# A two-layer trunk on one core: the seven products of each MLP weight pair put side by side, and the tiles of x and its sums moved in on-chip memory

## The chip, the cores and the metric

One core of a Trainium2 chip runs the whole program in one launch. The metric is the device time of one execution in microseconds (us), and of several executions the median. Nothing crosses cores, and the weights come from HBM once.

The engines are named as the profile names them. PE multiplies matrices; PEld is its weight load, which runs beside it. DVE and POOL do elementwise work, ACT applies functions and casts, and SP only issues loads and stores.

## The reference

Two layers work on 512 tokens of 1024 features. Each is a mixer (gated delta rule in the first, sliding-window attention in the second, both beside a small cross-attention) and an MLP. The change touches the MLP above all; the rest is shown by its names alone.

```python
def sq_relu_mlp(h, w_up, w_down):                  # h 512x1024, w_up 1024x4096, w_down 4096x1024
    return jnp.square(jax.nn.relu(h @ w_up)) @ w_down

def reference(x, mem, positions, a_w_in, ..., mlp_w_up, mlp_w_down, ln_g, ln_b):
    ...
    for layer in range(DEPTH):                     # DEPTH = 2
        mix = mixer_a(...) if layer < N_A else mixer_b(...)
        h = layer_norm(DN_ALPHA * h + mix, ln_g[layer, 0], ln_b[layer, 0])
        h = layer_norm(DN_ALPHA * h + sq_relu_mlp(h, mlp_w_up[layer], mlp_w_down[layer]), ...)
        if layer == N_A - 1:
            k_sh, v_sh = shared_kv(h, w_kv_shared, cos, sin)
    return h
```

## The kernel before, in words

**Split operands.** Every large matmul runs on numbers split into a high part (a cast to a shorter float, on ACT) and a low part (what is left, a subtraction on DVE). A product is then three matmuls: high by high, low by high, high by low. `wload` (line 81) loads a weight tile `wr` and splits it into `wh` and `wl`; `split_copy` (line 117) does the same for a tile that is there already. The activations stand in `XH` and `XL`, with features on the partitions. In a row `out<-a,b` of the views, one of a, b is the stationary operand (its 128 columns are loaded by PEld) and the other is the moving one (its 256 or 512 columns stream through PE).

**The MLP.** `mlp` (line 777) runs once per layer. The 4096 hidden features fall into eight chunks of 512, and a chunk into two pairs of 128-feature tiles. `ups_first` computes the first chunk, `ups_second` half of the second, and the 13 pairs that remain are objects of `Pair`, so there are 26 in the program. A pair multiplies a 2 by 2 arrangement of weight blocks by a 2 by 2 arrangement of x blocks with seven block products in place of eight. `x_sums` (line 833) builds the three sums of x blocks once per layer, as the split tiles `TH` and `TL`; `up_load` (line 854) loads a pair's two weight tiles and builds four weight sums `sa`, `sb` on POOL.

**The seven products.** `product` (line 865) issues 12 matmuls, 4 blocks of 128 features by 3, each with 256 moving columns. The results gather in three accumulators, `upa`, `upb` and `upd`, and a product that adds onto one of them may start only when the sum that has to read it before is done. That sets the order: m1 (opens `upa`), m6 (opens `upb`), then the sum u2 on DVE, m2 (onto `upa`), m5 (opens `upd`), m7 (onto `upb`), then the sums u3 and r22, m4 (onto `upb`), the sum r21, m3 (onto `upd`), the sum r12. m1, m2, m5 and m3 read `XH` and `XL`; m6, m7 and m4 read `TH` and `TL`. m4's weights are `w2h` and `w2l`, a small tile of their own; the other weights are `wh` and `wl`. `close` applies relu and square and splits the result into `hh` and `hl`.

**The downs.** `down` (line 938) multiplies an earlier chunk's `hh`, `hl` by a slab of the second weight matrix for one tile of 128 tokens: 12 matmuls of 512 moving columns into a bank `dn`, of which there are three, and one DVE addition onto `res`. A pair comes with four downs.

**The order of the work.** Each engine runs its queue in order. The loop in `mlp` gives the order of PE: m1, m6, m2, m5, m7, down 0, m4, down 1, m3, down 2, down 3. A scheduler may put elementwise work on the other engines earlier than the code does: the splits of the next pair (`split0` for the first weight tile, `split_b` and `split_a` for `sb` and `sa`, `split2` for `w2h`) stand between the current pair's sums. Weight tiles come in a ring of four `wr` and five `wh`, `wl`, so a load on SP waits until the tile that it overwrites has been split.

Of the kernel before, what the change touches and what calls it, by code (L numbers as in the profile page):

```python
# [11 lines left out]
F32 = mybir.dt.float32  # L12
# [6 lines left out]
P = 128  # L19
# [30 lines left out]
def trunk(ctx: ExitStack, tc: tile.TileContext, xT, xn, memT, wk, wq, wv, wqm, wz, wmk, wmv, wo0, wo1, up, dn,  # L50
# [15 lines left out]
    def ct(shape, tag, dt=F32):  # L66
        return cp.tile(shape, dt, tag=tag, name=tag)
# [7 lines left out]
    def fr(ap):  # L75
        return ap.bitcast(F32)
# [4 lines left out]
    def wload(src, shape):  # L81
# [6 lines left out]
        V.tensor_sub(lo, raw, fr(hi))  # L88
        return hi, lo

    XH = ct([P, KT, S], "XH", F32R)
    XL = ct([P, KT, S], "XL", F32R)
    res = ct([P, NT, D], "res")
    lns = ctx.enter_context(tc.tile_pool(name="lns", bufs=2))
    wa_stack = ExitStack()
    wpool[0] = wa_stack.enter_context(tc.tile_pool(name="wa", bufs=3))
# [19 lines left out]

    def split_copy(src, hi, lo):
        A.copy(hi, src)  # L118
        V.tensor_sub(lo, src, fr(hi))  # L119

    def split_scores(ps, q, k):

# [26 lines left out]
    triu = c0([P, P], "triu")  # L149
    G.affine_select(triu, ones, [[1, P]], ALU.is_ge, 0.0, base=0, channel_multiplier=-1)  # L150
    slow = c0([P, P], "slow", F32R)
    slow32 = c0([P, P], "slow32")
    G.affine_select(slow32, ones, [[-1, P]], ALU.is_gt, 0.0, base=0, channel_multiplier=1)
    V.tensor_copy(slow, slow32)
    mtri = c0([P, P], "mtri")
    G.memset(mtri, 0.0)
    G.affine_select(mtri, mtri, [[1, P]], ALU.is_ge, NEG, base=0, channel_multiplier=-1)
    band = ct([P, 256], "band")
# [8 lines left out]
    convw = ct([P, 18, 4], "convw")  # L167
    gbT = ct([P, 4, 2, KT], "gbT")

    def row_bcast(src, n, tag):  # L170
        t = ct([P, n], tag)
        SY.dma_start(t, src.rearrange("(o n) -> o n", o=1).broadcast_to([P, n]))
        return t

# [40 lines left out]
    SY.dma_start(gbT, lngb)  # L215
    alog_b = row_bcast(alog, NH, "alog_b")
    dtb_b = row_bcast(dtb, NH, "dtb_b")
    nw_b = row_bcast(nw, P, "nw_b")
    sink_b = row_bcast(sinks, 12, "sink_b")
    invf_b = row_bcast(invf, 32, "invf_b")  # L220
    pos_i = ct([P, NT], "pos_i", I32)
# [20 lines left out]
            if gates is not None:  # L242
                V.tensor_copy(gates[:, :, t], ps[:, n:n + 12])

    ab = ct([P, 12, NT], "ab")
    proj_z(2, ab)


    gg = [ct([P, 24], f"gate{i}") for i in range(12)]
    (ga, gb_, ge, gs, gs2, gacc, g_, beta, eg, neg, egl, gt) = gg  # L250

    def v6(t):
# [19 lines left out]
    for n in (13, 11, 9, 7, 5, 3, 1):  # L272
# [9 lines left out]
    gsp = [ct([P, 24], f"gsplit{i}", F32R) for i in range(2)]  # L282
    split_copy(g_, *gsp)
    ps = smt("v6ps")
    T.matmul(ps[:, 0:24], triu, g_, start=True, stop=True)
# [491 lines left out]
    def mlp(pool, layer, last, gb0):  # L777
# [5 lines left out]
        def f4(shape, n):  # L783
            return pool.tile(shape, F32, tag="f4", name=nm(n), bufs=5)

        def split(raw, shape, tag="wh"):
# [4 lines left out]
            split_copy(raw, hi, lo)  # L791
            return hi, lo

        def hidden(r, hh, hl):
# [38 lines left out]
        def x_sums():  # L833
            q = lambda k, t: (XH[:, k, t], XL[:, k, t])
            x11, x12, x21, x22 = q(kA, tA), q(kA, tB), q(kB, tA), q(kB, tB)
            t1 = f4([P, 4, HT], "t1")
            if layer == 0:
                f11, f12, f21, f22 = (xf[j][:, :, t] for j in range(2) for t in (tA, tB))
            else:
                f11, f12, f21, f22 = t1, *(f4([P, 4, HT], n) for n in ("f12", "f21", "f22"))  # L840
                for f, x in ((f11, x11), (f12, x12), (f22, x22), (f21, x21)):
                    V.tensor_tensor(f, fr(x[0]), fr(x[1]), op=ALU.add)
            V.tensor_sub(t1, f12, f11)
            V.tensor_sub(f12, f22, f12)
            V.tensor_sub(f22, f22, t1)
            V.tensor_sub(f21, f21, f22)
            TH, TL = (pool.tile([P, 3, 4, HT], F32R, tag=n, name=nm(n), bufs=1) for n in ("TH", "TL"))
            for i, t in enumerate((f22, f12, f21)):
                split_copy(t, TH[:, i], TL[:, i])

            xq.update(t1=t1, B11=x11, B21=x21, B22=x22, T1=x12,
                      **{n: (TH[:, i], TL[:, i]) for i, n in enumerate(("T2", "T3", "T4"))})
# [9 lines left out]
            G.tensor_tensor(sb[:, 1], raw[0][:, kB], sb[:, 0], op=ALU.subtract)  # L862
            return raw, sa, sb

        def product(ps, w, x, start, stop):
            (hi, lo), (mh, ml) = w, x
            for k in range(4):
                T.matmul(ps, hi[:, k, :], mh[:, k, :], start=start and k == 0, stop=False, skip_group_check=True)  # L868
                T.matmul(ps, hi[:, k, :], ml[:, k, :], start=False, stop=False, skip_group_check=True)  # L869
                T.matmul(ps, lo[:, k, :], mh[:, k, :], start=False, stop=stop and k == 3, skip_group_check=True)  # L870

        class Pair:
# [23 lines left out]

            def m1(self):
                self.a = smt("upa")[:, 0:HT]
                product(self.a, self.A11, xq["B11"], True, False)
                self.s1 = self.small("m1")  # L900
                A.copy(self.s1, self.a)

# [11 lines left out]
            def m7(self):  # L914
                product(self.b, self.S3, xq["T3"], False, False)
                self.u3 = self.small("u3")
                V.tensor_tensor(self.u3, self.s1, self.b, op=ALU.add)
                V.tensor_tensor(self.r[:, 1, tB], self.u3, self.d, op=ALU.add)

            def m5(self):  # L920
                self.d = smt("upd")[:, 0:HT]
                product(self.d, self.S1, xq["T1"], True, False)

            def m4(self):
                product(self.b, self.A22, xq["T4"], False, True)
# [48 lines left out]
        for c in range(NC - 1):  # L974
            later = new_hid()
            for n in range(2):
                p, nxt = nxt, None
                first = c == 0 and n == 0
                f0 = 4 * c + 2 * n + 6
                if first:  # L980
                    ups_second(later)
                    slabs = dn_slabs(c, n)
                else:
                    p.m1()
                    p.m6()
# [282 lines left out]
```

## Time and profile before

| | |
|---|---|
| time, median of 3 runs | 1182.09 us (1181.24 to 1185.84) |
| the profiled execution, its time and its span | 1183.56 us and 1181.8 us |
| ACT busy | 559.3 us (47%) |
| POOL busy | 220.7 us (19%) |
| weights read from HBM | 109.53 MB |
| mean granted clock of PE | 0.991 |

The span runs from the first to the last instruction; the time is 1.8 us longer. A matmul's busy time includes its way through the array, so that busy times of matmuls in a row overlap: how fast PE really goes is read from the distance between starts. The MLP of the first layer fills about 340 to 655 us of the span, that of the second about 840 to 1150 us; the mixers fill the rest.

### The profile page before, as it was taken

To read this page: it belongs to the slowest core of one execution; us is meant where nothing else is said; L and a number is where in the kernel's file an instruction comes from. 1 tells how busy PE (TensorE), PEld (TensorE's weight loads), DVE (VectorE), ACT (ScalarE), POOL (GpSimd) and SP (SyncE) were. 2 spreads that over 40 slices of the span, in tenths; PEclk is the share of its full clock that TensorE was granted. 3 is DMA by queue.
4 is the path that set the end of the run, shared out by engine and by line. 5 is a ranking of instruction groups with operands and counts; after the bars stand their busy time and mean duration, and the time that the engine had idled before them with its cause. 6 is when DMAs were issued, how large, how long until landed. Compare 5 with 4: busy or idle time off the path is not lost.

```text
span 1181.8 us, 18955 instructions
## 1 busy us (share of the span) xinstructions
PE 1153.5 (98%) x7470; PEld 1013.4 (86%) x7470; DVE 857.4 (73%) x1606; ACT 559.3 (47%) x1008; POOL 220.7 (19%) x180
## 2 busy tenths in 40 slices
PE   8999999999999999999999999999999999999996
PEld 8877788879998899898998887778988998989985
DVE  5478889777698676666666968886986666666657
ACT  6345454755384354544435236652653545444341
POOL 0112111101005322313110100000053223131104
PEclk9999999999999999999999999999999999999998
DMA  7522141203423323242333241102342232423311
GB/s 254 180 72 79 61 133 39 68 19 114 154 68 125 112 89 126 72 141 74 106 110 92 70 135 62 55 19 72 108 136 97 89 125 72 140 75 108 107 36 71
DMA packets 40729, 114.16 MB, mean 97 GB/s; under 512 B 11136, under 2 KB 12032, under 8 KB 40640
## 3 DMA queue, kind: packets, MB, share of 16 engines
q1 hardware_dynamic: 40064, 112.04, 29.4%
q8 instruction: 58, 0.95, 0.3%
q10 hardware_dynamic: 576, 0.92, 0.2%
q14 instruction: 31, 0.25, 0.1%
HBM read 109.53 MB, written 3.41 MB: 96 GB/s over the span
## 4 chain that ended last, share of the span: by engine, by line
PE 83%; DVE 10%; ACT 3%; DMA 1%; POOL 1%; issue 1%; POOLq 0%; SPq 0%; ACTq 0%; DVEq 0%
PE dn L113 9%; PE dn L114 9%; PE dn L112 9%; PE upb L868 3%; PE upb L869 3%; PE upb L870 3%; PE wo L114 2%; PE wo L112 2%; PE wo L113 2%; PE upa L869 2%; PE upd L869 2%; PE upa L870 2%; PE upd L870 2%; PE upa L868 2%; PE upd L868 2%; PE up L103 2%
## 5 line engine op out<-in xcount | busy, mean ns | idle before, releaser
L114 PE MATMUL dn<-wh,hl 128*128 128x512 f32 x512 | 200.0, 391 | 0.0
L113 PE MATMUL dn<-wl,hh 128*128 128x512 f32 x512 | 200.0, 391 | 0.0
L112 PE MATMUL dn<-wh,hh 128*128 128x512 f32 x512 | 199.6, 390 | 0.0
L87 ACT CAST wh<-wr 128x1024 fp32r<-128x1024 f32 (+1 forms) x136 | 142.5, 1051 | 104.4 <-PE dn L114 25.0
L88 DVE TENSOR_TENSOR wl<-wr,wh 128x1024 fp32r<-128x1024 f32 (+1 forms) x136 | 166.4, 1226 | 34.1 <-ACT wh L87 31.7
L947 DVE TENSOR_TENSOR res<-res,dn 128x512 f32<-128x512 f32 x120 | 82.1, 684 | 53.8 <-PE dn L114 53.7
L114 PEld LDWEIGHTS dn<-wh,hl 128*128 128x128 f32 x512 | 96.1, 188 | 20.3
L112 PEld LDWEIGHTS dn<-wh,hh 128*128 128x128 f32 x512 | 96.4, 188 | 17.6
L113 PEld LDWEIGHTS dn<-wl,hh 128*128 128x128 f32 x512 | 96.1, 188 | 17.7
L859 POOL TENSOR_TENSOR sa<-wr 128x512 f32<-128x512 f32 x26 | 39.2, 1506 | 373.8 <-DMA wr<-in_up_dram 306.2
L653 POOL TENSOR_TENSOR rs<-rs,nhalf 128x1 f32<-128x1 f32 x16 | 13.3, 833 | 334.9 <-DVE rs L652 267.7
L118 ACT CAST wh<-sa 128x1024 fp32r<-128x1024 f32 x26 | 27.3, 1050 | 90.2 <-PE upd L869 90.2
L119 DVE TENSOR_TENSOR wl<-wr,wh 128x1024 fp32r<-128x1024 f32 x26 | 33.0, 1268 | 43.9 <-ACT wh L118 43.9
L869 PE MATMUL upa<-XL,wh 128*128 128x256 f32 x208 | 58.5, 281 | 0.0
L869 PE MATMUL upd<-XL,wh 128*128 128x256 f32 x208 | 58.5, 281 | 0.0
L870 PE MATMUL upa<-XH,wl 128*128 128x256 f32 x208 | 58.4, 281 | 0.0
L870 PE MATMUL upd<-XH,wl 128*128 128x256 f32 x208 | 58.3, 280 | 0.0
L868 PE MATMUL upa<-XH,wh 128*128 128x256 f32 x208 | 58.3, 280 | 0.0
L868 PE MATMUL upd<-XH,wh 128*128 128x256 f32 x208 | 58.2, 280 | 0.0
L868 PE MATMUL upb<-TH,wh 128*128 128x256 f32 x208 | 58.0, 279 | 0.0
L869 PE MATMUL upb<-TL,wh 128*128 128x256 f32 x208 | 57.8, 278 | 0.0
L870 PE MATMUL upb<-TH,wl 128*128 128x256 f32 x208 | 57.6, 277 | 0.0
(402 smaller groups left out, 3296.7 us busy)
## 6 DMA issues: line engine op xcount, KB each, us to landing
wr<-in_up_dram SPq DMA_DIRECT2D x64, 512.0 KB, 4.8
wr<-in_dn_dram SPq DMA_DIRECT2D x64, 512.0 KB, 4.3
wr<-in_wo_dram SPq DMA_DIRECT2D x16, 512.0 KB, 3.6
wr<-in_bw_dram SPq DMA_DIRECT2D x8, 512.0 KB, 4.5
wr<-in_wz_dram SPq DMA_DIRECT2D x6, 520.0 KB, 4.4
wr<-in_wk_dram SPq DMA_DIRECT2D x6, 512.0 KB, 3.7
wr<-in_wq_dram SPq DMA_DIRECT2D x6, 512.0 KB, 3.6
wr<-in_wv_dram SPq DMA_DIRECT2D x6, 512.0 KB, 3.6
```

The costliest lines, as they stand in the source:

```text
L87: A.copy(hi, raw)
L88: V.tensor_sub(lo, raw, fr(hi))
L112: T.matmul(ps, sh, hi[:, kk, :], start=(k == 0), stop=False)
L113: T.matmul(ps, sh, lo[:, kk, :], start=False, stop=False)
L114: T.matmul(ps, sl, hi[:, kk, :], start=False, stop=(k == nk - 1))
L118: A.copy(hi, src)
L119: V.tensor_sub(lo, src, fr(hi))
L859: G.tensor_tensor(sa[:, 0], raw[1][:, kA], raw[1][:, kB], op=ALU.add)
L868: T.matmul(ps, hi[:, k, :], mh[:, k, :], start=start and k == 0, stop=False, skip_group_check=True)
L869: T.matmul(ps, hi[:, k, :], ml[:, k, :], start=False, stop=False, skip_group_check=True)
L870: T.matmul(ps, lo[:, k, :], mh[:, k, :], start=False, stop=stop and k == 3, skip_group_check=True)
L947: V.tensor_tensor(dst, dst, ps, op=ALU.add)
```

## The change

Four things change.

1. **Order of the products.** All seven run one after the other (m1, m6, m2, m7, m5, m4, m3), and then the four downs. The sum r22 moves from `m7` to `m5`, which now comes later.
2. **The first split of the next pair.** `split0` may not go ahead of r22 on DVE any more: `behind` adds an order between the two, without a semaphore.
3. **Places in memory.** Small unused tiles (`pad0` to `pad4`) and the move of some small mixer tiles to the other end of the memory shift the large tiles. The table has, for the tiles that PE reads, the start in a partition's bytes, as the program's allocation has it, divided by 256: the remainder.
4. **A copy of the first block of x.** Once per layer ACT copies the 256 columns of `XH` that m1 reads first into a tile `x0`, and the first matmul of each m1 reads that copy. Its remainder differs from that of `XH` by 32.

| tile | remainder before | after |
|---|---|---|
| `XH`, `XL`, `res` | 128 | 160 |
| `TH`, `TL` | 160 | 160 |
| `wh`, `wl` of the MLP | 224 | 224 |
| `w2h`, `w2l` | 160 | 224 |
| `hh`, `hl` | 224 | 224 |
| `x0` | none | 128 |
| `MH`, `ML` (memory tokens, at the start) | 224 | 224 |
| the four `wh` of the first mixer | 32, 224, 160, 96 | 32, 224, 160, 96 |

Since every step inside these tiles that a matmul's start takes is a multiple of 256, the remainder holds for all blocks of a tile.

```diff
+    ct([P, 8], "pad0")
     XH = ct([P, KT, S], "XH", F32R)
     XL = ct([P, KT, S], "XL", F32R)
     res = ct([P, NT, D], "res")
+    ct([P, 56], "pad1")
...
     def split_copy(src, hi, lo):
         A.copy(hi, src)
-        V.tensor_sub(lo, src, fr(hi))
+        return V.tensor_sub(lo, src, fr(hi))
+
+    def behind(ins, first):
+
+        if first is not None:
+            tc.add_manual_dep(ins.ins, first.ins.name,
+                              mybir.DependencyInfo(mybir.DependencyClass.NoSync, mybir.DependencyReason.DATA),
+                              reason="order")
...
     slow = c0([P, P], "slow", F32R)
-    slow32 = c0([P, P], "slow32")
-    G.affine_select(slow32, ones, [[-1, P]], ALU.is_gt, 0.0, base=0, channel_multiplier=1)
-    V.tensor_copy(slow, slow32)
     mtri = c0([P, P], "mtri")
+    G.affine_select(mtri, ones, [[-1, P]], ALU.is_gt, 0.0, base=0, channel_multiplier=1)
+    V.tensor_copy(slow, mtri)
     G.memset(mtri, 0.0)
...
-    ab = ct([P, 12, NT], "ab")
+    ab = c0([P, 12, NT], "ab")
...
             for i, t in enumerate((f22, f12, f21)):
                 split_copy(t, TH[:, i], TL[:, i])
+
+            pool.tile([P, 40], F32, tag="pad3", name=nm("pad3"), bufs=1)
+            xq["first"] = pool.tile([P, HT], F32R, tag="x0", name=nm("x0"), bufs=1)
+            pool.tile([P, 24], F32, tag="pad4", name=nm("pad4"), bufs=1)
+            A.copy(xq["first"], fr(XH[:, 0, tA]))
...
-        def product(ps, w, x, start, stop):
+        def product(ps, w, x, start, stop, first=None):
             (hi, lo), (mh, ml) = w, x
             for k in range(4):
-                T.matmul(ps, hi[:, k, :], mh[:, k, :], start=start and k == 0, stop=False, skip_group_check=True)
+                m = mh[:, k, :] if k or first is None else first
+                T.matmul(ps, hi[:, k, :], m, start=start and k == 0, stop=False, skip_group_check=True)
...
-            def split0(self):
-                hi, lo = split(self.raw[0], [P, KT, P])
+            def split0(self, first):
+                hi, lo = split(self.raw[0], [P, KT, P], first=first)
...
                     p.m2()
+                    p.m7()
                     p.m5()
-                    p.m7()
+                    p.m4()
+                    p.m3()
+                    p.close(later)
...
                 down(c, 0, n, hid, slabs)
-                if not first:
-                    p.m4()
                 if nxt:
-                    nxt.split0()
+                    nxt.split0(None if first else p.r22)
                 down(c, 1, n, hid, slabs)
-                if not first:
-                    p.m3()
-                    p.close(later)
```

The tables below show rows of the built programs; lines are those of each kernel's own source, so `L868` before is `L884` after, and `L112` is `L115`.

On PE, at the end of m7 in the sixth pair of the first layer, before: the last matmuls of m7 (`upb`), then down 0.

```order
L868 MATMUL upb_4820<-TH_3703,wh_4787 128x256
L869 MATMUL upb_4820<-TL_3704,wh_4787 128x256
L870 MATMUL upb_4820<-TH_3703,wl_4788 128x256
L112 MATMUL dn_4903<-wh_4841,hh_4213 128x512
L113 MATMUL dn_4903<-wl_4842,hh_4213 128x512
L114 MATMUL dn_4903<-wh_4841,hl_4214 128x512
```

The same place in the change: m7 ends, and m5 (`upd`) follows at once.

```order
L884 MATMUL upb_4826<-TH_3704,wh_4793 128x256
L885 MATMUL upb_4826<-TL_3705,wh_4793 128x256
L886 MATMUL upb_4826<-TH_3704,wl_4794 128x256
L884 MATMUL upd_4885<-XH,wh_4793 128x256
L885 MATMUL upd_4885<-XL,wh_4793 128x256
L886 MATMUL upd_4885<-XH,wl_4794 128x256
```

Where m1 begins, the change has `x` (the copy) in the place of `XH`, in one matmul of the twelve.

```order
L116 MATMUL dn_4797<-wl_4658,hh_4219 128x512
L117 MATMUL dn_4797<-wh_4657,hl_4220 128x512
L884 MATMUL upa_4811<-x_502_3714,wh_4757 128x256
L885 MATMUL upa_4811<-XL,wh_4757 128x256
L886 MATMUL upa_4811<-XH,wl_4758 128x256
```

On DVE, the same pair from the sum u2 on, before: u2 (`L907`), `split0` of the next pair (`wl<-wr`), u3 and r22 (`L917`, `L918`), `split_b`, the addition of down 0, r21 (`L926`), and so on.

```order
L907 TENSOR_TENSOR u_665_4833<-m_663_4818,upb_4820 128x256
L119 TENSOR_TENSOR wl_4931<-wr_4893,wh_4930 128x1024
L917 TENSOR_TENSOR u_676_4890<-m_663_4818,upb_4820 128x256
L918 TENSOR_TENSOR r_4863<-u_676_4890,upd_4865 128x256
L119 TENSOR_TENSOR wl_4966<-sb_4898,wh_4965 128x1024
L947 TENSOR_TENSOR res<-res,dn_4903 128x512
L926 TENSOR_TENSOR r_4863<-m_663_4818,upb_4820 128x256
L119 TENSOR_TENSOR w2l_5250<-wr_5112,w2h_5249 128x512
L947 TENSOR_TENSOR res<-res,dn_4934 128x512
L930 TENSOR_TENSOR r_4863<-u_665_4833,upd_4865 128x256
L119 TENSOR_TENSOR wl_4984<-sa_4897,wh_4983 128x1024
```

After: the three sums u2, u3, r22 stand together, `split0` comes behind them, and the additions of the downs come behind all five sums.

```order
L923 TENSOR_TENSOR u_669_4839<-m_667_4824,upb_4826 128x256
L933 TENSOR_TENSOR u_679_4883<-m_667_4824,upb_4826 128x256
L938 TENSOR_TENSOR r_4869<-u_679_4883,upd_4885 128x256
L122 TENSOR_TENSOR wl_4954<-wr_4929,wh_4953 128x1024
L942 TENSOR_TENSOR r_4869<-m_667_4824,upb_4826 128x256
L122 TENSOR_TENSOR wl_4972<-sb_4934,wh_4971 128x1024
L946 TENSOR_TENSOR r_4869<-u_669_4839,upd_4885 128x256
L122 TENSOR_TENSOR wl_4990<-sa_4933,wh_4989 128x1024
L963 TENSOR_TENSOR res<-res,dn_4939 128x512
L122 TENSOR_TENSOR w2l_5256<-wr_5148,w2h_5255 128x512
L122 TENSOR_TENSOR hl_4614<-r_4869,hh_4613 128x1024
```

On ACT the cast of `w2h` moves from ahead of the relu to behind the square, in 22 pairs; the other engines' queues hold the same work in the same order, but for the two copies and the mask `mtri` at the start.

More of the change, by code (lines that the diff above doesn't have):

```diff
@@ L168, in trunk, with row_bcast @@
     gbT = ct([P, 4, 2, KT], "gbT")
-    def row_bcast(src, n, tag):
-        t = ct([P, n], tag)
+    def row_bcast(src, n, tag, where=ct):
+        t = where([P, n], tag)
         SY.dma_start(t, src.rearrange("(o n) -> o n", o=1).broadcast_to([P, n]))
@@ L217, in trunk @@
     dtb_b = row_bcast(dtb, NH, "dtb_b")
-    nw_b = row_bcast(nw, P, "nw_b")
+    nw_b = row_bcast(nw, P, "nw_b", c0)
     sink_b = row_bcast(sinks, 12, "sink_b")
@@ L243, in proj_z @@
                 V.tensor_copy(gates[:, :, t], ps[:, n:n + 12])
-    ab = ct([P, 12, NT], "ab")
+    ab = c0([P, 12, NT], "ab")
     proj_z(2, ab)
-    gg = [ct([P, 24], f"gate{i}") for i in range(12)]
+    gg = [c0([P, 24], f"gate{i}") for i in range(12)]
     (ga, gb_, ge, gs, gs2, gacc, g_, beta, eg, neg, egl, gt) = gg
@@ L281, in trunk @@
                            op0=ALU.mult, op1=ALU.mult)
-    gsp = [ct([P, 24], f"gsplit{i}", F32R) for i in range(2)]
+    gsp = [c0([P, 24], f"gsplit{i}", F32R) for i in range(2)]
     split_copy(g_, *gsp)
@@ L784, in f4, with split @@
             return pool.tile(shape, F32, tag="f4", name=nm(n), bufs=5)
-        def split(raw, shape, tag="wh"):
+        def split(raw, shape, tag="wh", first=None):
             small = tag != "wh"
@@ L790, in split @@
             lo = wp.tile(shape, F32R, tag=tag[:-1] + "l", name=nm(tag[:-1] + "l"), bufs=n)
-            split_copy(raw, hi, lo)
+            behind(split_copy(raw, hi, lo), first)
             return hi, lo
@@ L847, in x_sums @@
             TH, TL = (pool.tile([P, 3, 4, HT], F32R, tag=n, name=nm(n), bufs=1) for n in ("TH", "TL"))
+            pool.tile([P, 16], F32, tag="pad2", name=nm("pad2"), bufs=1)
             for i, t in enumerate((f22, f12, f21)):
                 split_copy(t, TH[:, i], TL[:, i])
+            pool.tile([P, 40], F32, tag="pad3", name=nm("pad3"), bufs=1)
+            xq["first"] = pool.tile([P, HT], F32R, tag="x0", name=nm("x0"), bufs=1)
+            pool.tile([P, 24], F32, tag="pad4", name=nm("pad4"), bufs=1)
+            A.copy(xq["first"], fr(XH[:, 0, tA]))
             xq.update(t1=t1, B11=x11, B21=x21, B22=x22, T1=x12,
@@ L898, in m1 @@
                 self.a = smt("upa")[:, 0:HT]
-                product(self.a, self.A11, xq["B11"], True, False)
+                product(self.a, self.A11, xq["B11"], True, False, xq["first"])
                 self.s1 = self.small("m1")
@@ L917, in m7 @@
                 V.tensor_tensor(self.u3, self.s1, self.b, op=ALU.add)
-                V.tensor_tensor(self.r[:, 1, tB], self.u3, self.d, op=ALU.add)
             def m5(self):
@@ L922, in m5 @@
                 product(self.d, self.S1, xq["T1"], True, False)
+                self.r22 = V.tensor_tensor(self.r[:, 1, tB], self.u3, self.d, op=ALU.add)
             def m4(self):
```

## The prediction

> **What bounds the kernel now.** I read the page first: the span, the shares of the engines, the granted clock by slices, and the chain of waits.
>
> ```profile
> span 1181.8 us, 18955 instructions
> PE 1153.5 (98%) x7470; PEld 1013.4 (86%) x7470; DVE 857.4 (73%) x1606; ACT 559.3 (47%) x1008; POOL 220.7 (19%) x180
> PEclk9999999999999999999999999999999999999998
> PE 83%; DVE 10%; ACT 3%; DMA 1%; POOL 1%; issue 1%; POOLq 0%; SPq 0%; ACTq 0%; DVEq 0%
> ```
>
> PE is busy 98% of the span at a full clock, and 83% of the chain is PE itself. So taking waits away can bring little; a large gain has to make PE faster at the same 7470 matmuls. Whether there is room is read from the distance between starts. The groups give the counts, the timeline of one late pair the distances.
>
> ```profile
> L112 PE MATMUL dn<-wh,hh 128*128 128x512 f32 x512 | 199.6, 390 | 0.0
> L868 PE MATMUL upa<-XH,wh 128*128 128x256 f32 x208 | 58.3, 280 | 0.0
> L102 PE MATMUL kq<-XH,wh 128*128 128x512 f32 x96 | 38.5, 401 | 0.0
> L102 PE MATMUL up<-XH,wh 128*128 128x256 f32 x128 | 36.0, 282 | 0.0
> L112 PE MATMUL projqMM<-wh,XH 128*128 128x512 f32 x64 | 25.9, 405 | 0.0
> L102 PE MATMUL up<-XH,wh 128*128 128x512 f32 x32 | 12.7, 396 | 0.0
> ```
>
> ```profile
> 376.77 0.28 PE L868 MATMUL upa<-XH,wh 128*128 128x256 f32 x1
> ...
> 605.72 0.28 PE L868 MATMUL upa<-XH,wh 128*128 128x256 f32 x1
> ...
> 607.14 0.28 PE L868 MATMUL upb<-TH,wh 128*128 128x256 f32 x1
> ...
> 608.51 0.28 PE L868 MATMUL upa<-XH,wh 128*128 128x256 f32 x1
> ...
> 609.92 0.28 PE L868 MATMUL upd<-XH,wh 128*128 128x256 f32 x1
> ...
> 611.33 0.28 PE L868 MATMUL upb<-TH,wh 128*128 128x256 f32 x1
> ...
> 612.72 0.39 PE L112 MATMUL dn<-wh,hh 128*128 128x512 f32 x1
> ...
> 615.46 0.28 PE L868 MATMUL upb<-TH,w2h 128*128 128x256 f32 x1
> ...
> 616.88 0.39 PE L112 MATMUL dn<-wh,hh 128*128 128x512 f32 x1
> ...
> 619.65 0.28 PE L868 MATMUL upd<-XH,wh 128*128 128x256 f32 x1
> ...
> 621.08 0.39 PE L112 MATMUL dn<-wh,hh 128*128 128x512 f32 x1
> ...
> 623.81 0.39 PE L112 MATMUL dn<-wh,hh 128*128 128x512 f32 x1
> ...
> 626.53 0.28 PE L868 MATMUL upa<-XH,wh 128*128 128x256 f32 x1
> ```
>
> Eleven pairs begin between 376.77 and 605.72, at 20.81 us each, and the next takes 20.81 too: every pair is alike, and none has a gap. Within a pair each product is twelve equal matmuls, yet m1 takes 1.42 us, m6 1.37, m2 1.41, m5 1.41, m7 1.39, m4 1.43, m3 1.43: 9.86 in all. The two that read TH with a `wh` tile are the shortest. The downs take 2.74, 2.77, 2.73 and 2.72.
>
> The only thing in the tables that goes with it is the pair of remainders. XH at 128 with weights at 224 gives 1.41 / 12 = 117.5 ns from start to start; TH at 160 with 224 gives 1.37 / 12 = 114.2, the way in included; `w2h` at 160 with TH at 160, together with the way in from a down, 1.43 / 12 = 119. The start of the program has the same products with other remainders:
>
> ```profile
> 14.54 0.28 PE L114 MATMUL VM<-wh,ML 128*128 128x256 f32 x1
> ...
> 16.66 0.28 PE L112 MATMUL VM<-wh,MH 128*128 128x256 f32 x1
> ...
> 18.32 0.28 PE L104 MATMUL KM<-MH,wl 128*128 128x256 f32 x1
> ...
> 19.52 0.28 PE L102 MATMUL KM<-MH,wh 128*128 128x256 f32 x1
> 19.88 0.28 PE L102 MATMUL KM<-MH,wh 128*128 128x256 f32 x1
> ...
> 22.48 0.28 PE L104 MATMUL KM<-MH,wl 128*128 128x256 f32 x1
> ```
>
> KM's line is one loop. While its weights lie at 224, as MH does, ten steps take 1.20 us (120 ns); from the buffer at 160 on, 23 steps take 2.60 (113). So 113.3 is what PE can do (12 of them 1.36 us), and equal remainders cost 6.7 ns a matmul. VM is a warning: its weights at 32 differ from ML's 224 by an odd multiple of 64, as TH from `wh`, and still 18 steps take 2.12 (117.8). A fitting difference is thus not enough; the stream must also fall into step, and TH's products, which come behind a product at another remainder, do.
>
> **The change part by part.**
>
> *Places of XH and w2.* They take XH to TH's remainder, so that m1, m2, m5 and m3 meet `wh` as m6 and m7 do, and take `w2h` to where `wh` lies. This operation is not in the trace: no XH product at 160. Bounds: 113.3 ns at best, 120 at worst (KM at equal remainders). I take 113.3, since TH with `wh` has both remainders of the new case.
>
> *All seven products contiguous.* There is then one way in per pair, at m1, from a down. `x0`, 32 away, is read by the first matmul only. Its price is not shown; the nearest row is m7, which comes from XH to TH and takes 1.39 against 1.36, so 0.03; bounds 0 and 0.07 (m4, from a down). The downs follow one another: the second and the third lose 0.05 and 0.01, and the first keeps its 0.02.
>
> New pair: 7 x 1.36 + 0.03 + 4 x 2.72 + 0.02 = 20.45. Gain 0.36 each, 26 x 0.36 = 9.4 us.
>
> *XH elsewhere.* The first chunk's matmuls and the second's, of the second layer:
>
> ```profile
> 849.73 0.28 PE L104 MATMUL up<-XH,wl 128*128 128x256 f32 x1
> ...
> 851.14 0.28 PE L104 MATMUL up<-XH,wl 128*128 128x256 f32 x1
> ...
> 859.70 0.40 PE L102 MATMUL up<-XH,wh 128*128 128x512 f32 x1
> ...
> 862.51 0.40 PE L102 MATMUL up<-XH,wh 128*128 128x512 f32 x1
> ```
>
> Twelve steps take 1.41 and 2.81, against 1.36 and 2.72: 4.2 and 7.5 ns a matmul. The group of 128 stands for 3 x 128 / 2 = 192 matmuls in one layer: 0.8 us. I count one layer, since PE idles in the first one's. The group of 32 stands for 96: 0.7. In the mixers kq has 288 and projq 192 at about 7.5 ns too, 2.2 and 1.4 us at most, but their weights change remainder from buffer to buffer; bounds 0 and 3.6, and I take 1.4.
>
> *The sums.* Four products in a row on one accumulator leave less time to the sums between. From DVE's timeline:
>
> ```profile
> 381.19 0.41 DVE L907 TENSOR_TENSOR u<-m,upb 128x256 f32<-128x256 f32 x1
> ...
> 608.78 0.42 DVE L907 TENSOR_TENSOR u<-m,upb 128x256 f32<-128x256 f32 x1 [0.18 <-PE upb L870]
> 611.09 1.23 DVE L119 TENSOR_TENSOR wl<-wr,wh 128x1024 fp32r<-128x1024 f32 x1 [1.88 <-ACT wh L118]
> 612.92 0.42 DVE L917 TENSOR_TENSOR u<-m,upb 128x256 f32<-128x256 f32 x1 [0.60 <-PE upb L870]
> ```
>
> u2 ends at 609.20; m7, which waits for it, would now start at 605.72 + 0.03 + 3 x 1.36 = 609.83: 0.63 to spare. u3 ends 0.62 behind the last start of m7 (613.34 against 612.72), and m4 comes one product later, 1.36: 0.74 to spare, and r22 before m3 likewise. These hold only if DVE is free at that time: the 1.23 us of `split0` between u2 and u3 would use all of it, and the new order keeps it out. The first pair is the exception: u2 ends at 381.60 there, and m7 would start at 376.77 + 4.11 = 380.88, a stall of 0.7 us. In the second layer's first pair I expect at most that, and take 0.
>
> *Behind `split0`.* It ended at 612.32, 6.6 us into the pair; behind r22 (612.55 + 0.62) it ends at about 614.4, 8.7 in. SP's next load of that tile, which waits for it, goes 2 us later, and all loads behind it in SP's queue. What reads the load is POOL:
>
> ```profile
> 449.59 1.30 POOL L859 TENSOR_TENSOR sa<-wr 128x512 f32<-128x512 f32 x1 [13.64 <-DMA wr<-in_up_dram]
> ...
> 471.93 1.87 DVE L119 TENSOR_TENSOR w2l<-wr,w2h 128x512 fp32r<-128x512 f32 x1
> ```
>
> It stands 10.4 us into the fourth pair (376.77 + 3 x 20.81 = 439.20). At 12.4, four such sums end by 17.6, inside the pair, and the splits of `sa` and `sb` stand behind the sums of the pair that follows. No PE wait is seen: I cost this at nothing. ACT's cast of `w2h`, moved behind the square, precedes its use by most of a pair; the copies into `x0` are two, ahead of 26 pairs: nothing.
>
> Sum: -9.4 - 0.8 - 0.7 - 1.4 + 0.7 = -11.6 us. On the profiled execution, 1183.56 (span 1181.8 and 1.8 around it), that is 1172.0; it lies 1.5 above the median of the runs, from which it would be 1170.5. I say 1171.
>
> **The rivals.**
>
> *Places do nothing here (it doesn't do what it says).* The distances would then come from something that moves with the order, and stay: only the 0.7 of the first pair remains, 1183. Against it: KM, where only the weight buffer changes. The Trainium skill, in "SBUF — State Buffer", section "SBUF: two separate sides", says that on the engines' side only the port pair shared by DVE and GpSimd causes contention and that PE never waits; by that rule no place could matter. KM's 120 and 113 ns speak against it here. In "TensorE: Matmul & The Clock Gate", section "Wait — 56ns, not 53.3ns?", it has a fixed cost of about 2.5 ns per matmul on N / 2.4 GHz, which gives an estimate of 109.2 ns for 256 columns; no row here reaches it.
>
> *Partial: XH's products stay out of step,* as VM does at a fitting difference. Then only m4 (0.07) and the downs (0.06) gain: 26 x 0.13 = 3.4, less 0.7: 1179. For it: VM. Against: all of m6 and m7.
>
> *Wrong step, the slower side.* If the row of 84 locks at the 120 ns of KM's first part, it has no product at another remainder in it any more to leave that state: 84 x 0.120 = 10.08 against 9.86, +0.22, downs -0.06, 26 x 0.16 = 4.2; the first chunk 192 x 2.5 ns, 0.5; the stall 0.7. Together +5.4: 1187.5. With the downs' gain it decides at (9.86 + 0.06) / 84 = 118.1 ns a matmul: from there on the pair is longer than before. For it: one wrong way in is carried through the whole row, where now each change of operand ends it.
>
> *DVE late at u2.* POOL's sums stretch DVE's work: w2l took 1.87 where half of the 1.23 would be 0.62. One such stretch ahead of u2, from 0.63 on, stalls PE by 0.6 in a pair; in all 26 that is +16, less 11.6: +4, 1186. Against it: POOL is busy 19%, and its sums end before the next pair's u2.
>
> **How the numbers follow.** Forecast 0.70; places do nothing 0.05; partial 0.10; wrong step 0.08; DVE late 0.07. The forecast alone has 1167 (mixers whole, no way in, no stall) to 1176 (mixers nothing, dearer ways in, a stall per layer). The range reaches on to 1183, taking in the partial case and that of no effect: 1167 to 1183, with the last two cases, 0.15, above. What a measurement of this kernel tells from no change is about 0.5%, 5.9 us, or 1176.2 to 1188. The forecast is faster, with the 0.01 of the partial case that gets as far: 0.71. The two slower cases, 1187.5 and 1186, lie right at the bound of 1188, so I give half of them to each side of it: slower 0.08, and same 0.09 partial, 0.05 nothing and 0.07, which is 0.21.
>
> **What would show it.** Starts of m1 in the changed trace 20.45 apart: right; 20.8: places do nothing; 21.0: wrong step. Twelve steps of m2, m5 and m3 in 1.36 each: the places; m1 near 1.39: the way in. A `PE` row of m7 or m4 with idle time before it, released by `u`: DVE late, expected once, at the first pair. `sa` about 12.4 into a pair: the later load. kq at 390 ns in the groups: the mixers' whole 2.2. The forecast is wrong if XH's products show 117 or more.

## The result, and the profile after

| | before | after |
|---|---|---|
| median of 7 runs, us | 1182.09 (1178.74 to 1185.84) | 1170.9 (1169.27 to 1177.4) |
| ratio, 95% interval | | 0.9914 (0.9887 to 0.9941) |
| span of the profiled execution, us | 1181.8 | 1169.2 |
| distance of m1 to the next pair's m1, us | 20.81 | 20.43 |

A second set of runs of both kernels gave 1182.12 and 1172.56, ratio 0.9926 (0.9903 to 0.995). The page after, same lines as before:

```profile
span 1169.2 us, 18962 instructions
PE 1137.7 (97%) x7470; PEld 1000.1 (86%) x7470; DVE 860.7 (74%) x1606; ACT 555.8 (48%) x1010; POOL 242.5 (21%) x180
PEclk9999999999999999999999999999999999999998
PE 76%; DVE 15%; ACT 3%; DMA 2%; issue 2%; POOL 1%; POOLq 0%; SPq 0%; ACTq 0%; DVEq 0%
```

The same 7470 matmuls at the same clock, PE busy 15.8 us less and the span 12.6 us shorter: PE runs faster, it doesn't wait less. The timeline of PE (start and duration in us, engine, line, what) for the twelfth pair of the first layer shows where:

```profile
599.59 0.28 PE L884 MATMUL upa<-x,wh 128*128 128x256 f32 x1
...
600.97 0.28 PE L884 MATMUL upb<-TH,wh 128*128 128x256 f32 x1
...
602.33 0.28 PE L884 MATMUL upa<-XH,wh 128*128 128x256 f32 x1
...
603.69 0.28 PE L884 MATMUL upb<-TH,wh 128*128 128x256 f32 x1
...
605.05 0.28 PE L884 MATMUL upd<-XH,wh 128*128 128x256 f32 x1
...
606.41 0.28 PE L884 MATMUL upb<-TH,w2h 128*128 128x256 f32 x1
...
607.77 0.28 PE L884 MATMUL upd<-XH,wh 128*128 128x256 f32 x1
...
609.13 0.39 PE L115 MATMUL dn<-wh,hh 128*128 128x512 f32 x1
...
620.02 0.28 PE L884 MATMUL upa<-x,wh 128*128 128x256 f32 x1
```

m1 takes 1.38 us and the six behind it 1.36 each, where before they took 1.37 to 1.43; the four downs take 10.89 against 10.96. The granted clock is 1.00 in both kernels from the first pair to the last, so the clock isn't the reason. 23 of the 26 pairs are like this. The first of all has the longest wait of PE in this part of the program:

```profile
373.04 0.28 PE L884 MATMUL upa<-x,wh 128*128 128x256 f32 x1
...
375.78 0.28 PE L884 MATMUL upa<-XH,wh 128*128 128x256 f32 x1
...
378.79 0.39 PE L884 MATMUL upb<-TH,wh 128*128 128x256 f32 x1 [1.49 <-DVE u L923]
...
380.28 0.28 PE L884 MATMUL upd<-XH,wh 128*128 128x256 f32 x1
```

m2 and the wait behind it take 3.01 us in place of 1.36, and m7 1.49: the wait costs 1.65, and coming in again 0.13.

The last pair of each layer has a short one. In the thirteenth, DVE does the split of a tile that `wload` has loaded (`L88`), which `behind` doesn't hold back, between u2 and u3:

```profile
625.30 1.23 DVE L88 TENSOR_TENSOR wl<-wr,wh 128x1024 fp32r<-128x1024 f32 x1 [1.84 <-ACT wh L87]
626.44 0.41 DVE L933 TENSOR_TENSOR u<-m,upb 128x256 f32<-128x256 f32 x1
```

```profile
626.91 0.38 PE L884 MATMUL upb<-TH,w2h 128*128 128x256 f32 x1
```

u3 ends at 626.85, and m4 starts at 626.91, 0.07 us behind m5's end. With the coming in again (m4 takes 1.47) that is 0.17 us, and 0.19 in the last pair of the second layer.

By the starts of the same matmul in both traces, the 12.6 us come in four stretches: 2.3 up to the first projection of the first mixer (35.85 to 33.56), 1.4 from there to the first pair (376.77 to 373.04), 4.2 from there to the first pair of the second layer (879.03 to 871.13), and 4.7 to the end.

### The profile page after: what moved, and what is told of

It reads as the page before. It is cut to its first block, busy times and chain, and to the rows that moved or that the text cites. A ratio compares the mean times of both kernels' runs of the same rounds, so it can differ in the third digit from the quotient of the medians.

```text
span 1169.2 us, 18962 instructions
## 1 busy us (share of the span) xinstructions
PE 1137.7 (97%) x7470; PEld 1000.1 (86%) x7470; DVE 860.7 (74%) x1606; ACT 555.8 (48%) x1010; POOL 242.5 (21%) x180
## 4 chain that ended last, share of the span: by engine, by line
PE 76%; DVE 15%; ACT 3%; DMA 2%; issue 2%; POOL 1%; POOLq 0%; SPq 0%; ACTq 0%; DVEq 0%
PE dn L116 9%; PE dn L117 9%; PE dn L115 9%; PE upb L884 3%; PE upb L885 3%; PE upb L886 3%; PE wo L117 2%; DVE wl L88 2%; PE wo L115 2%; PE wo L116 2%; PE upd L885 2%; PE upd L884 2%; PE upd L886 2%; PE upa L885 2%; PE upa L884 2%; PE upa L886 2%
## 5 line engine op out<-in xcount | busy, mean ns | idle before, releaser
L88 DVE TENSOR_TENSOR wl<-wr,wh 128x1024 fp32r<-128x1024 f32 (+1 forms) x136 | 166.3, 1225 | 77.7 <-ACT wh L87 77.0
L115 PE MATMUL dn<-wh,hh 128*128 128x512 f32 x512 | 199.5, 390 | 0.0
L115 PEld LDWEIGHTS dn<-wh,hh 128*128 128x128 f32 x512 | 96.1, 188 | 19.0
L884 PE MATMUL upb<-TH,wh 128*128 128x256 f32 x208 | 57.5, 277 | 1.5 <-DVE u L923 1.5
L122 DVE TENSOR_TENSOR hl<-r,hh 128x1024 fp32r<-128x1024 f32 x26 | 56.1, 2156 | 1.9 <-ACT hh L121 1.9
L884 PE MATMUL upd<-XH,wh 128*128 128x256 f32 x208 | 57.4, 276 | 0.0
L875 POOL TENSOR_TENSOR sb<-sa,wr 128x512 f32<-128x512 f32 x26 | 57.4, 2207 | 0.0
L121 ACT CAST wh<-wr 128x1024 fp32r<-128x1024 f32 x26 | 27.4, 1053 | 53.5 <-PE upa L885 53.5
```

Of the source, the lines that this page charges most:

```text
L115: T.matmul(ps, sh, hi[:, kk, :], start=(k == 0), stop=False)
L122: return V.tensor_sub(lo, src, fr(hi))
L875: G.tensor_tensor(sb[:, 0], sa[:, 0], raw[0][:, kA], op=ALU.subtract)
L884: T.matmul(ps, hi[:, k, :], m, start=start and k == 0, stop=False, skip_group_check=True)
```

## The experiments

All eleven runs were profiled, and all but two (the map and the repeat of the kernel before) timed several times. Times within a few us of each other overlap, so the verdicts rest on the rows.

**The order alone.** The kernel of before with m7 ahead of m5, m4 and m3 ahead of the downs, r22 in m5 and `split0` behind it; all tiles where they were, no `x0`.

```diff
...
                     p.m2()
-                    p.m5()
                     p.m7()
+                    p.m5()
+                    p.m4()
+                    p.m3()
+                    p.close(later)
...
```

> The new order and the later split, with all tiles where they were before and no x0. If the places make the gain: m1, m2, m5 and m3 stay at 1.41 to 1.42 us (117.5 ns a matmul), m4 at 1.43, m6 and m7 at 1.37 to 1.39, pair 20.75 us; with the stall of the first pair the time is about 1181 to 1183. If the row itself makes it: pair 20.43 to 20.5, time 1171 to 1174.

Measured: 1181.2 us, ratio 0.9989 (0.9974 to 1.0003). The end of the row in the twelfth pair:

```profile
605.02 0.28 PE L874 MATMUL upb<-TH,wh 128*128 128x256 f32 x1
...
606.43 0.28 PE L874 MATMUL upd<-XH,wh 128*128 128x256 f32 x1
...
607.86 0.28 PE L874 MATMUL upb<-TH,w2h 128*128 128x256 f32 x1
...
609.30 0.28 PE L874 MATMUL upd<-XH,wh 128*128 128x256 f32 x1
```

m7 1.41, m5 1.43, m4 1.44; pair 20.79. What the downs gain, m7 and m5 give back. In the pairs the order alone brings 26 x 0.02 = 0.5 us.

**The places alone.** The changed kernel with the order of before, and m1 reading `XH`.

```diff
-                product(self.a, self.A11, xq["B11"], True, False, xq["first"])
+                product(self.a, self.A11, xq["B11"], True, False)
...
-                    p.m7()
                     p.m5()
-                    p.m4()
-                    p.m3()
-                    p.close(later)
+                    p.m7()
...
```

> The new places with the order of before, m1 reading XH instead of the copy. If places alone are enough: every product 1.36 to 1.39 us, pair 20.45 to 20.6, time 1170 to 1174. If a row must come in over a matmul at another remainder: after a down all products run at 120 ns, 1.44 us each, pair 84 x 0.120 + 10.95 = 21.0, 5 us more than before in the pairs less some 3 gained elsewhere: 1183 to 1186.

Measured: 1179.95 us, ratio 0.9971 (0.9957 to 0.9985).

```profile
603.90 0.28 PE L884 MATMUL upa<-XH,wh 128*128 128x256 f32 x1
...
605.32 0.28 PE L884 MATMUL upb<-TH,wh 128*128 128x256 f32 x1
...
606.73 0.28 PE L884 MATMUL upa<-XH,wh 128*128 128x256 f32 x1
```

Every product takes 1.41 us, 117.7 ns a matmul, m6 and m7 too, which were the fast ones before; pair 20.77, 26 x 0.04 = 1.0 us less than before. Neither number expected came: the places don't suffice, and a row that hasn't come into step runs at 117.7, as VM did (117.8), not at 120.

**The copy without its displacement.** The changed kernel with 32 bytes moved from behind `x0` to ahead of it.

```diff
-            pool.tile([P, 40], F32, tag="pad3", name=nm("pad3"), bufs=1)
+            pool.tile([P, 48], F32, tag="pad3", name=nm("pad3"), bufs=1)
...
-            pool.tile([P, 24], F32, tag="pad4", name=nm("pad4"), bufs=1)
+            pool.tile([P, 16], F32, tag="pad4", name=nm("pad4"), bufs=1)
```

> The changed kernel with the copy x0 at remainder 160, as XH, in place of 128. If the first matmul's displacement brings the row into step: without it all 84 products stay at 120 ns (1.44 us a product), pair 10.08 + 10.90 = 20.98, 26 x 0.55 = 14 us over the changed kernel: 1184 to 1186. If places alone are enough: pair 20.43 or a little less, 1170 to 1172.

Measured: 1180.64 us, ratio 0.9979 (0.997 to 0.9989).

```profile
602.88 0.28 PE L884 MATMUL upa<-x,wh 128*128 128x256 f32 x1
...
604.29 0.28 PE L884 MATMUL upb<-TH,wh 128*128 128x256 f32 x1
...
612.77 0.39 PE L115 MATMUL dn<-wh,hh 128*128 128x512 f32 x1
...
623.65 0.28 PE L884 MATMUL upa<-x,wh 128*128 128x256 f32 x1
```

Seven products take 9.89 us, 1.41 each, and the pair 20.77. Nothing else differs from the changed kernel: 32 bytes in the operand of one matmul in 84 are worth 0.34 us a pair, 8.8 us in all. The 120 ns that this expectation counted with didn't come.

**w2 back at 160.** The changed kernel with `pad4` 64 bytes shorter.

```diff
-            pool.tile([P, 24], F32, tag="pad4", name=nm("pad4"), bufs=1)
+            pool.tile([P, 8], F32, tag="pad4", name=nm("pad4"), bufs=1)
```

> The changed kernel with w2h and w2l back at remainder 160. If only the place of a product's own operands counts: m4 1.43 to 1.44 us, m3 behind it 1.36 to 1.39, pair 20.51 to 20.55, time 1173 to 1174. If equal remainders throw what follows out of step too: m3 1.41 to 1.44 as well, pair 20.6. If the place of w2 does nothing: pair 20.43, 1171.

Measured: 1176.88 us, ratio 0.9936 (0.9913 to 0.9959).

```profile
608.73 0.28 PE L884 MATMUL upd<-XH,wh 128*128 128x256 f32 x1
...
610.09 0.28 PE L884 MATMUL upb<-TH,w2h 128*128 128x256 f32 x1
...
611.52 0.28 PE L884 MATMUL upd<-XH,wh 128*128 128x256 f32 x1
...
612.94 0.39 PE L115 MATMUL dn<-wh,hh 128*128 128x512 f32 x1
```

m5 still 1.36, m4 1.43 and m3 1.42: equal remainders throw the row out of step, and it stays out. Pair 20.59, 0.16 x 26 = 4.2 us.

**Without the order on DVE.** `split0` may stand ahead of r22 again.

```diff
-                    nxt.split0(None if first else p.r22)
+                    nxt.split0(None)
```

> The changed kernel without the order between r22 and the next pair's first split: the split's 1.23 us of DVE stand between u2 and u3 again. If u3 and r22 have only the 0.74 us to spare that was worked out: m4 waits for u3 up to 0.5 us and m3 for r22 less or nothing, pair 20.6 to 20.9, time 1175 to 1184. If the split fits between u2's end and the end of m7 (it has two products of 1.36 us there): pair 20.43, time 1171.

Measured: 1176.12 us, ratio 0.9944 (0.9924 to 0.9964). DVE in the twelfth pair:

```profile
607.71 1.23 DVE L122 TENSOR_TENSOR wl<-wr,wh 128x1024 fp32r<-128x1024 f32 x1 [1.84 <-ACT wh L121]
608.86 0.41 DVE L933 TENSOR_TENSOR u<-m,upb 128x256 f32<-128x256 f32 x1
```

The split waits for ACT's cast until 607.71, u3 stands behind it and ends at 609.27; m4 starts at 609.32, 0.07 behind m5's end, and takes 1.47 while it comes in again. Pair 20.62, 0.19 x 26 = 4.8 us. The wait itself is the smaller half of it.

**m5 first, in the first pair alone.** So that one more product stands ahead of the one that waits for u2. `m5(False)` leaves r22 to `sum22`, behind m7.

```diff
...
+                    early = layer == 0 and c == 0
+                    if early:
+                        p.m5(False)
                     p.m7()
-                    p.m5()
+                    if early:
+                        p.sum22()
+                    else:
+                        p.m5()
```

> The changed kernel with m5 ahead of m7 in the first pair of the first layer alone, so that one more product stands between u2's product and the one that waits for u2. If DVE's backlog alone makes the stall: it falls from 1.65 us to about 0.3, the span by 1.4, time 1169 to 1170; the other pairs stay at 20.43. If the stall only moves to another sum of that pair: no gain, 1171.

Measured: 1172.14 us, ratio 0.9908 (0.9888 to 0.9927), not told apart from the changed kernel's. The first pair takes 21.05 us where the changed kernel's two traces have 22.21 and 21.52; the others 20.43. PE's wait for u2 fell to 0.27 us, as the first case has it. The other 0.35 lie in the products behind it: m7 1.47, m4 1.50 and m3 1.41, with three matmuls of a down between m7 and m4, which the edit doesn't show.

**Two rows.** The changed kernel with down 0 between m5 and m4, and a second copy, also 32 bytes off, for m4's first matmul.

```diff
-                    p.m4()
-                    p.m3()
-                    p.close(later)
...
                 down(c, 0, n, hid, slabs)
+                if not first:
+                    p.m4()
+                    p.m3()
+                    p.close(later)
```

> The changed kernel with the first down between m5 and m4, and a second displaced copy, which m4's first matmul reads. If a way in over a displaced matmul is what counts, and not that all seven are contiguous: m4 1.38 us as m1, all others 1.36, pair 20.43 + 0.02 + 0.02 = 20.47, time 1171 to 1173. If one contiguous row is needed: m4 and m3 at 1.41, pair 20.54 to 20.6, 1174 to 1176.

Measured: 1170.37 us, ratio 0.9903 (0.9879 to 0.9926).

```profile
605.10 0.39 PE L115 MATMUL dn<-wh,hh 128*128 128x512 f32 x1
...
607.83 0.28 PE L886 MATMUL upb<-x,w2h 128*128 128x256 f32 x1
...
609.21 0.28 PE L886 MATMUL upd<-XH,wh 128*128 128x256 f32 x1
...
610.57 0.39 PE L115 MATMUL dn<-wh,hh 128*128 128x512 f32 x1
```

m4 1.38 and m3 1.36, pair 20.47, as worked out. That the seven are contiguous saves one way in, 0.03 us a pair; it isn't what makes them fast. One pair of this trace, the seventh, took 21.43:

```profile
491.16 2.00 DVE L122 TENSOR_TENSOR wl<-sa,wh 128x1024 fp32r<-128x1024 f32 x1
...
496.06 1.73 DVE L88 TENSOR_TENSOR wl<-wr,wh 128x1024 fp32r<-128x1024 f32 x1
```

```profile
499.91 0.39 PE L886 MATMUL upb<-TH,wh 128*128 128x256 f32 x1 [0.67 <-DVE u L925]
```

While POOL's sums ran (489.04 to 496.70) two splits took 2.00 and 1.73 us in place of 1.21 to 1.23; u2 came late and m7 waited. It is the prediction's rival "DVE late at u2", in one pair.

**A map of the places.** A kernel of its own, with nothing but rows of 24 matmuls.

```python
steps = [(512, 56, 56)] * 4                       # columns, moving and stationary place in 4-byte words
if shift:
    steps.append((n, (r + 56) % 64, s))           # one matmul 32 bytes off
steps += [(n, r, s)] * 24
```

> Leaves the reference's computation out altogether and measures only: rows of 24 matmuls of 256 moving columns for each of 8 by 8 remainders (steps of 32 bytes) of moving and stationary operand, behind four of 512 columns, once straight and once behind one matmul whose moving operand is 32 bytes off; then 512 columns for some. If the state theory holds: 160 with 224 gives 117.7 ns straight and 113.3 displaced, equal remainders 120 either way, 128 with 224 117 to 119 either way; and what holds for 160 with 224 holds for every pair with the same difference. If the absolute place counts, rows with the same difference differ.

Worked out from its trace: mean distance of starts over the last 17 steps of a row, in ns, 256 columns, behind a displaced matmul.

```
moving \ stationary    0     32     64     96    128    160    192    224
  0                 120.0  118.2  113.3  117.5  118.4  120.3  117.8  116.8
 32                 116.5  120.0  118.2  113.3  117.5  118.4  120.2  117.8
 64                 117.8  116.5  120.0  118.2  113.4  118.6  118.8  119.7
 96                 119.9  117.8  116.6  120.0  118.5  117.7  118.6  120.2
128                 118.9  120.2  117.8  116.9  120.0  118.2  113.3  118.6
160                 117.5  118.5  119.7  117.8  117.9  120.0  118.2  113.3
192                 117.8  118.5  119.9  120.0  113.4  116.9  120.0  118.2
224                 118.2  113.4  117.3  118.9  120.2  117.8  116.5  119.6
```

Equal remainders take 120. A stationary operand 64 bytes above the moving one takes 113.3 or 113.4 in six of eight rows; the other two (96 with 160 and 192 with 0) stayed at 117.7 and 117.8. So the expectation that all pairs with this difference behave alike failed for two of eight. Straight behind the four matmuls of 512 columns only two of those eight came into step, 64 with 128 and 128 with 192, and 160 with 224 took 117.7. A stationary operand 64 bytes below came to 113.4 once, 192 with 128; 224 with 160, which KM had at 113 in the program, took 117.8 in the map. The places of `XH` before (128 with 224) took 118.9 straight and 118.6 behind a displaced matmul: there the displacement brings next to nothing. So, as far as the map goes, the difference decides whether 113.3 can be had, and the way in whether it is; why two of the eight rows didn't come in, it doesn't show. At 512 columns it is the other way about: 160 with 160 took 226.9 and 224 with 224 226.6, a stationary operand 64 below (160 with 96, 224 with 160) 228.9, and 160 with 224 233.3, all straight.

**The mixer's weights at 160.** The kernel with m5 first, the gate weights loaded in four tiles of half the size, which brings all weight buffers of the first mixer to 160.

```diff
-        slabs = [wload(wz[zg, kh], [P, 4, CW]) for kh in range(2)]
+        slabs = [wload(wz[zg, kh][:, 2 * j:2 * j + 2], [P, 2, CW]) for kh in range(2) for j in range(2)]
```

> The kernel with m5 first in the first pair, and the first mixer's weight buffers all at remainder 160 (its gate weights in four tiles of 4 KB in place of two larger ones, so that the ring has one step). By the map, 512 moving columns go at 226.7 ns where both remainders are equal: kq, v and qm from 230.8 to about 227, some 400 x 4 ns = 1.6 us on PE; KM rises or falls by less than 0.3. If PE is what ends last in the first mixer: 1.5 us less up to the MLP, time 1167 to 1169. If the mixer is bound by the other engines' chain: kq at 227 and no gain in time, 1169 to 1171.

Measured: 1173.75 us, ratio 0.9931 (0.991 to 0.9951). The distances of kq (mean of those under 245 ns) fell from 230.9 to 227.1 ns, as the map has it, yet the first pair starts at 374.87 against 372.21 and 373.04 in the changed kernel's traces. The granted clock isn't the reason: from the first projection to the first pair it was 0.98, and this stretch took 341.03 us against 339.42 to 339.50 in the four traces of the new places that had 0.98 as well. So 3.8 ns less for each matmul of kq brought no gain in time. The edit also makes twelve loads and splits out of six, so the run doesn't show what the places alone would bring.

**Both kernels once more,** unchanged, to see which stages vary by themselves.

> The changed kernel unchanged. If the 2.3 us gained ahead of the first projection belong to the change: the projection starts at 33.5 us again. If they are a matter of the single run: it starts anywhere from 33 to 37, as in the other runs. Pair 20.43, time 1170 to 1172.

> The kernel of before unchanged, for its stages in a second run. If its start is always the slow one: the first projection begins at 35.9 us again and the first mixer's output at 273. If stages outside the MLP vary from run to run: other values by up to some us. Pair 20.81 either way.

Measured: 1172.56 us, ratio 0.9926 (0.9903 to 0.995), for the changed kernel, its pairs at 20.43; 1183.62, a single run, for that of before, its pairs at 20.81. The first projection starts at 33.63 in the one and 36.67 in the other. Two rows of a table by stretches (length, busy time and count on PE, PEld, DVE, ACT, POOL, then the granted clock, the DMAs' share and GB/s), the changed kernel's first trace and the second of before:

```profile
9.00:12.00 3.00, 2.65 (x23) 2.63 (x23) 2.86 (x5) 2.18 (x3) 1.88 (x3) 1.00 0.76 251
```

```profile
9.00:12.00 3.00, 2.70 (x9) 2.18 (x10) 2.83 (x5) 2.25 (x5) 0.00 (x0) 0.50 0.61 212
```

PE got its full clock in the one and half of it in the other: 23 matmuls against 9. Taken alone, the repeat of the changed kernel came out as its first case has it, at 33.6 again. What speaks for the single run are the other kernels that have the changed start. The granted clock from 6 to 16 us, and where the first projection began:

| granted clock, 6 to 16 us | traces | first projection, us |
|---|---|---|
| 1.00 | the changed kernel, twice | 33.56 and 33.63 |
| 0.83 | eight: two with the start of before, six with the changed one | 33.84 to 36.04 |
| 0.66 | the second of before; w2 at 160, with the changed start | 36.67 and 36.98 |

The changed start stands in all three rows, so it doesn't bring the early beginning by itself; the clock that a run got goes with it. What spreads the eight over 2 us, and whether the change has a smaller part in it, isn't shown.

## Why the prediction was right

- **The places and the way in** (9.4 us by the sum) were right: 20.45 was forecast for a pair, 20.43 measured, 26 x 0.38 = 9.9. The way in at m1 cost 0.02, not 0.03. The reason for `x0`, which the prediction took from VM and from how TH's products come in, is shown by moving its displacement alone. The order of before with the displaced copy wasn't run; the kernel "Two rows" shows that an interrupted row does as well if each part of it has a displaced matmul at its head. One thing the prediction didn't part: in KM and VM, its models, the stationary operand lies 64 bytes below the moving one, in the change 64 above. Only TH with `wh` had the right side; by the map, 64 below came into step in one row of eight.
- **The rivals.** That places do nothing falls with the kernels that move only pads. What the Trainium skill says in "SBUF — State Buffer", section "SBUF: two separate sides", that only the shared port pair causes contention and that PE never waits on anyone, doesn't cover this. Here the same operands 32 or 64 bytes elsewhere took 113.3, 117.7 or 120 ns. The partial case is what one gets without the displacement, or without the order, though then m6 and m7 fall to 117.7 as well. The wrong step exists, but at 117.7 ns, not at the 120 of KM's first part: KM had equal remainders, and 160 with 224 doesn't come to 120 in any run. 117.7 is just under the 118.1 ns from which, by the prediction, a pair gets longer than before: without the displacement the kernel took 1180.64 us, not 1187.5. The price was too high because it was taken from a row with other remainders.
- **The sums.** Spare times of 0.63 and 0.74 us were worked out. In the twelfth pair:

```profile
602.60 0.42 DVE L923 TENSOR_TENSOR u<-m,upb 128x256 f32<-128x256 f32 x1
...
605.25 0.42 DVE L933 TENSOR_TENSOR u<-m,upb 128x256 f32<-128x256 f32 x1 [2.23 <-PE upb L886]
606.61 0.42 DVE L938 TENSOR_TENSOR r<-u,upd 128x256 f32<-128x256 f32 x1 [0.94 <-PE upd L886]
```

  u2 ends at 603.02 and m7 starts at 603.69, 0.67 later; u3 at 605.67 and m4 at 606.41, 0.74; r22 at 607.03 and m3 at 607.77, 0.74. In the changed kernel's two traces DVE is late at u2 in the first pair alone, so the rival of a wait in all pairs falls; "Two rows" has it once more, in one pair. At u3 DVE is late in the last pair of each layer, 0.17 and 0.19 us, together 0.4, which the prediction didn't have.
- **The first pair's stall** was forecast as 0.7 and cost 1.8 (1.1 in the second trace): a term mis-sized. It was worked out as if PE reached the pair when it did before. But PE got there 3.7 us earlier, and u2, behind DVE's own backlog, only 2.9:

```profile
377.19 1.21 DVE L88 TENSOR_TENSOR wl<-wr,wh 128x1024 fp32r<-128x1024 f32 x1
378.33 0.41 DVE L923 TENSOR_TENSOR u<-m,upb 128x256 f32<-128x256 f32 x1
```

  u2 ended at 378.74 against 381.60. The rest is the coming in again, 0.13, which the sum didn't have.
- **Behind `split0`.** POOL's first sum was forecast about 12.4 us into a pair. In the fifth pair:

```profile
469.06 1.31 POOL L874 TENSOR_TENSOR sa<-wr 128x512 f32<-128x512 f32 x1 [12.65 <-DMA wr<-in_up_dram]
```

  The pair begins at 456.56: 12.5. In the second to the sixth pair it is 12.2 to 13.6, and no wait of PE comes from it.
- **XH elsewhere** (2.9 us by the sum). The first chunk's part held and the second's didn't:

```profile
840.76 0.28 PE L107 MATMUL up<-XH,wl 128*128 128x256 f32 x1
...
842.12 0.28 PE L107 MATMUL up<-XH,wl 128*128 128x256 f32 x1
...
850.66 0.40 PE L106 MATMUL up<-XL,wh 128*128 128x512 f32 x1
...
853.46 0.40 PE L106 MATMUL up<-XL,wh 128*128 128x512 f32 x1
```

  Twelve steps of 256 columns take 1.36 in place of 1.41, as forecast; twelve of 512 take 2.80 in place of 2.81. The step that failed is "4.2 and 7.5 ns a matmul": it gave the 512-column matmuls the places of the 256-column ones, and the map shows that they want equal remainders. 0.7 became 0.1. In the first mixer kq went from 401 to 399 ns in the groups, and only 0.3 us of it show between the first projection (2.3 us ahead) and the mixer's output (2.6 ahead). From the first projection to the first pair the new places gain 0.5 to 1.5 us where the granted clock is the same: 340.92 with the old places and 339.42 to 339.50 with the new at 0.98, 339.20 and 337.98 to 338.66 at 0.99, 336.14 and 334.93 at 1.00. Outside the pairs and the start, 2.6 us were gained in place of 2.9.
- **The start** was not in the sum: 2.3 us ahead at the first projection. It goes with the granted clock of that run, and kernels with the same start began as late as 36.98.

So the profiled gain is 9.9 - 1.8 - 0.4 + 2.6 + 2.3 = 12.6 us, of which the start's 2.3 go with the granted clock of that run; 11.2 by the medians of the first set of runs, 9.6 by those of the second, against 11.6 by the sum. The mechanism was right, but that the first median lies 0.1 us from 1171 is partly luck: without the start the parts add up to 10.3.

What stays open is why a difference of 64 bytes, and why a displaced matmul; no run here shows it.

## What to carry to other kernels

Where PE is dense, read the distance from start to start for each product, not its duration, and set it against where its two operands lie: with 256 moving columns a stationary operand 64 bytes above the moving one gave 113.3 ns in six places of eight and equal remainders 120, with 512 columns equal remainders were best. A row of matmuls keeps the step in which it comes in, so one matmul 32 bytes off at its head can be worth more than the order of all the others; test such a change with its parts taken out, since in the pairs the order alone was worth 0.5 us here, the places alone 1.0, and both with the displaced matmul 9.9. When PE is made faster in one stage, work out anew at what time it meets the other engines' backlog.

## What was not expected of the hardware

- The same product on the same places runs at 113.3 or at 117.7 ns, and stays there for as long as nothing disturbs it: 84 matmuls in 23 of the 26 pairs here, 24 in the map.
- A wait of PE decides anew. With the copy at 160 every pair ran at 117.7 but the end of the first, behind its wait for u2:

```profile
378.69 0.39 PE L884 MATMUL upb<-TH,wh 128*128 128x256 f32 x1 [0.67 <-DVE u L923]
...
380.17 0.28 PE L884 MATMUL upd<-XH,wh 128*128 128x256 f32 x1
...
381.53 0.28 PE L884 MATMUL upb<-TH,w2h 128*128 128x256 f32 x1
```

  m7 takes 1.48 and m5 1.36: the wait brought the row into step, without any displaced matmul.
- From 6 to 16 us the granted clock was 1.00, 0.83 or 0.66 by the run, and the first projection began between 33.56 and 36.98 us. From there to the first pair the same places took 334.93 us at a granted clock of 1.00, 337.98 to 338.66 at 0.99 and 339.42 to 339.50 at 0.98, more than the change gains in that stretch.
